# First conv unit reordered, forms loaded in another order, border frames turned in pairs

## Chip, core and metric

The kernel runs on one core of a Trainium2 chip. The core has a matrix engine (TensorE, PE in the profile, with its weight loads as PEld), a vector engine (VectorE, DVE), a scalar engine (ScalarE, ACT), a general engine (GpSimd, POOL) and an engine that mainly issues transfers (SyncE, SP; its transfers show as SPq). Each engine works through its own list of instructions in order and waits on semaphores for the others. Matrix products are gathered in PSUM, everything else lies in SBUF or in the chip's memory (DRAM).

The metric is the device time of one execution in microseconds (us), less is better. Before the change the median of three runs was 2408.08 us (2403.67, 2408.08, 2408.69).

## What is computed

One step of a streaming encoder layer on 576 frames: 512 of a new stream ("prompt") and 64 of a running one ("sample"), width 2048. Cut to what matters here:

```python
hn = rmsnorm(x, g_norm1)
q, k, v, gb, gc, hc = split(hn @ w_in)          # 3 x 1024 for attention, 3 x 1024 for the conv
o_attn = stick_breaking attention of q, k, v (8 heads x 128, with cached keys and values)
u = gc * hc
conv = conv_w[0]*u[t-2] + conv_w[1]*u[t-1] + conv_w[2]*u[t]   # causal, 3 taps, with carried state
o_conv = gb * conv
mix = concat(rmsnorm(o_attn, g_attn_out), rmsnorm(o_conv, g_conv_out))
x = x + mix @ w_out
h2 = rmsnorm(x, g_norm2)
y = x + (silu(h2 @ w_gate) * (h2 @ w_up)) @ w_down            # w_gate, w_up: 2048 x 5632
```

All values are float32, and the outputs are y for both streams, the new keys and values, and the conv states.

## The kernel before

**Splits and units.** A float32 product is made of three matmuls. Each operand is split into a high half (ACT casts it to the type fp32r that PE multiplies) and a low half (DVE subtracts the high half): `split`, L222 to L224. PE then multiplies high by high, low by high and high by low. The 576 frames lie as two halves of 288 columns. From the third conv group on, large projections are done in "units": a 2 x 2 scheme in the manner of Strassen and Winograd, in which weight blocks a11, a12 (first half of the columns of a unit) and a21, a22 (second half) take part in seven products in place of eight. A product `(n, p)` of unit n is 24 matmuls (8 blocks of depth by 3) of 128x128 by 128x288. Its weight operand is a block or a sum of blocks:

- product 1: a11, product 2: a12, product 4: a22
- product 6: s1 - a11 with s1 = a21 + a22, product 5: s1, product 7: a21 - a11
- product 3: a12 less what product 6 used

The frames' operands are sums of the frames' blocks ("forms") made ahead of time. Products 1, 6, 5 and 3 add up in the same PSUM bank psy (`st["y"]`); between them ACT copies the partial sum out (`kept`, L1016: p1 after product 1, u2 after product 6, the copy named acc after product 5). Product 2 gathers in bank z0 (psx), products 7 and 4 in psw. `done` (L1031, L1033) evicts a result on DVE: it adds the kept part and scales by the row scale R1.

**Stages.** Heads (projection and attention), two conv groups in the standard way, then the conv units with number 0 to NCU - 1 = 8 (kinds u, u, b in turn: h, c and gate columns), then eight "output" units from NCU on, which multiply the attention half of the mix by w_out, then the conv half by w_out (`out_proj`), then units of w_gate and w_up, then units of w_down.

**The loop around the change** is over `corder`, the list of products of the conv and output units. In each turn `conv_run` issues product number k, and then `conv_prepare` makes the weight operand of number k + 4: sums on DVE (L975, L976, L977, L979), the high half on ACT, the low half on DVE. For unit 0 the list begins (0,1), (0,2), (1,1), (1,2), (0,6), (0,7), (0,5), (0,3), (0,4), and then (1,6), (1,7), (1,5). Products 1 and 2 of unit 0 are prepared in the group before, and those of unit 1 ahead of the loop. Weights come through three places of 1 MB; when the last sum of a block has been made (after the preparation of product 3 or 4), its place is given free and the next block is called into it (`call_columns`, L943, loads at L956 and L963). In unit 0, the preparation of product 6 makes all three sums at once, s1 into a spare block `cx`.

The order of ACT's and DVE's instructions is normally set by the planner of the tile framework from costs that it estimates; within a `manual_schedule` region an engine takes them in the order of the program's text. `start_mode` is such a region for ACT and DVE. It is opened ahead of the loop and closed after (1,2). `turn_mode` is another one, for SP, from (NCU - 1, 1) on.

**Forms of the output units.** In unit NCU - 1, after its products 6, 7 and 4, pairs of forms of the attention half are loaded (`load_forms`, L1072): forms 1 and 2, then 6 and 7, then 5 and 3, and form 4 last. Between these, in the preparation of (NCU - 1, 3), the place of that unit's first block is given free, and a block of w_out is called into it (L956).

**Stores of y.** In the last stage `take_blocks(d)` gives every down unit d its four blocks of sums, one for each column block c and half of the frames i. When a block is complete, `store_y` turns it: three PE transposes, two of 128 frames and one of the 32 frames left over (the border), a copy on ACT back over the block, a copy of the border into a small tile `obs` (L1688), then the stores. With 32 blocks that makes 32 turns of a border of 32 frames. Each half has its own.

The functions that the change touches:

Of the kernel before, what the change touches and what calls it, by code (L numbers as in the profile page):

```python
# [10 lines left out]
F32 = mybir.dt.float32  # L11
# [83 lines left out]
def tile_hybrid_stream_step(  # L95
# [872 lines left out]
    def conv_prepare(n, p_):  # L968
        st, tt, m = cst.setdefault(n, {"left": 7}), nc.vector.tensor_tensor, NP if n < NCU else NH // 2
        if p_ == 1:  # L970
            _, st["a11"], st["a12"] = cregion[n, 0]
        if p_ == 6:
            _, st["a21"], st["a22"] = cregion[n, 1]
            s1 = st["s1"] = bt["s1"][:, :m]
            tt(out=s1, in0=st["a21"], in1=st["a22"], op=ALU.add)  # L975
            tt(out=st["a21"], in0=st["a21"], in1=st["a11"], op=ALU.subtract)  # L976
            tt(out=st["a11"], in0=s1, in1=st["a11"], op=ALU.subtract)  # L977
        if p_ == 3:
            tt(out=st["a12"], in0=st["a12"], in1=st["a11"], op=ALU.subtract)  # L979
        src = st[{1: "a11", 2: "a12", 3: "a12", 4: "a22", 5: "s1", 6: "a11", 7: "a21"}[p_]]  # L980
# [9 lines left out]
    ft = {}  # L990

    def conv_frames(n, p_, j):
# [611 lines left out]
    acc = {}  # L1604
    down = {}

    def take_blocks(d):

        if d in (0, 1, 3):
            spare_block({0: "z", 1: "t", 3: "ax"}[d])  # L1610
        if d in (0, 3):
            four = [down["z"][:, q, :] for q in (range(4) if d == 0 else range(4, 6))]
            if d:
                four += [down["ax"][:, q, :] for q in range(2)]
        elif d < 3:
            t = down["t"] if d == 1 else ypool.tile([P, 4, HALF], F32, tag=f"y{NP - 1}", name=f"acc{d}")
            four = [t[:, q, :] for q in range(4)]
        elif d < 6:
            four = [pool.tile([P, HALF], F32, tag=tag, name=f"acc{d}", bufs=2)
                    for pool, tag in (((tmp, "y"), (tmp, "r")) if d == 4 else ((tmp, "sq"), (h2pool, "hx")))  # L1620
                    for _ in range(2)]
        else:
            pool, tag = (tmp, "hl") if d == 6 else (rpool, "R")
            two = [pool.tile([P, 2, HALF], F32, tag=tag, name=f"acc{d}", bufs=2) for _ in range(2)]
            four = [t[:, q, :] for t in two for q in range(2)]
        for q, ap in enumerate(four):
            acc[d, q // 2, q % 2] = ap

# [33 lines left out]
    def store_y(n, c, i):  # L1662
# [13 lines left out]
        quick = n == NU - 1  # L1676

        def work():
            yield 4 if quick else 9
            po = misc("pot")[:, : 3 * P]  # L1680
            for q in range(3):
                w = min(P, HALF - q * P)
                nc.tensor.transpose(po[:w, q * P : (q + 1) * P], src[:, q * P : q * P + w], ident)
            yield 0 if quick else 3
            ob = src[:, : 2 * P].rearrange("p (i c) -> p i c", c=P)
            nc.scalar.copy(out=ob, in_=po[:, : 2 * P].rearrange("p (i c) -> p i c", c=P))
            obs = down["pool"].tile([r, P], F32, tag="obs", name="obs", bufs=4)
            nc.scalar.copy(out=obs, in_=po[:r, 2 * P :])  # L1688
            yield 0 if quick else 4
            if i == 0:  # L1690
                nc.sync.dma_start(out=yp[: 2 * P, cs].rearrange("(i p) c -> p i c", p=P), in_=ob)
            else:
                put(f0, ob[:, 0, :])
                put(f0 + P, ob[:, 1, :])
            put(f0 + 2 * P, obs, nc.scalar if quick else nc.sync)

# [79 lines left out]
```

## Time and profile before

| | before |
|---|---|
| median of three runs | 2408.08 us |
| profiled execution, its own time | 2407.74 us |
| span, from its first to its last instruction | 2406.0 us |
| granted TensorE clock, mean | 0.997 |
| PE busy | 2373.6 us (99%) |
| DVE busy | 1898.7 us (79%) |
| ACT busy | 1168.1 us (49%) |
| POOL busy | 279.1 us (12%) |

How to read the lines that follow. A row of the timeline gives the start in us from the span's start, the duration (of the whole run of instructions when they are several), the engine, the line of the kernel, the operation, out<-in by the program's tile names, the shape and the count. In brackets stands how long the engine had been idle, and what released it. A row of the waits gives the engine and line, what it waited for, and the total, number of times and longest, in us. A row of the stretches gives a stretch's length, then each engine's busy time and count, then the granted clock as a share of full speed, the share of the DMA engines that were busy, and GB/s. whl is a pair of high and low halves, raw_a and raw_c are weight blocks, part is a kept partial sum, cv an evicted result.

### The profile page before, as it was taken

How to read it: one execution, taken by the hardware profiler on the slowest of the kernel's cores; microseconds unless marked ns; L12 is line 12 of the kernel's file. 1: busy time of each engine (PE TensorE's matmuls, PEld its weight loads, DVE VectorE, ACT ScalarE, POOL GpSimd, SP SyncE). 2: the span in 40 equal slices, each digit the busy share in tenths (PEclk: the TensorE clock that was granted, in tenths of full speed). 3: DMA queues.
4: the chain of work that ended last, by engine and by line, in shares of the span. 5: the costliest groups of instructions: out<-in, count | busy, mean ns of one | idle time of the engine just before them, and what ended most of it. 6: DMA issues, size and time to landing. Idle time of an engine off the chain costs nothing.

```text
span 2406.0 us, 44164 instructions
## 1 busy us (share of the span) xinstructions
PE 2373.6 (99%) x17825; PEld 2360.9 (98%) x17825; DVE 1898.7 (79%) x2854; ACT 1168.1 (49%) x2099; POOL 279.1 (12%) x384
## 2 busy tenths in 40 slices
PE   8999999989999999999999999999999999999999
PEld 8999999989999999999999999999999999999998
DVE  7767676678887768888888888888888777887875
ACT  6656565444444545444444444444444444444454
POOL 1111111231111120000000000000000001431211
PEclk9999999999999999999999999999999999999999
DMA  7354433584268733444444434534444945885642
GB/s 255 116 153 138 136 118 95 180 285 123 88 206 221 212 120 112 138 145 150 137 133 150 152 117 155 160 113 156 150 129 141 337 137 189 231 233 196 203 128 80
DMA packets 503956, 386.04 MB, mean 160 GB/s; under 512 B 11726, under 2 KB 492872, under 8 KB 503752
## 3 DMA queue, kind: packets, MB, share of 16 engines
q1 hardware_dynamic: 494408, 366.68, 47.8%
q0 software_dynamic: 8624, 16.22, 3.3%
q8 instruction: 139, 2.28, 0.4%
q14 instruction: 65, 0.53, 0.1%
q10 hardware_dynamic: 720, 0.33, 0.0%
HBM read 296.47 MB, written 86.72 MB: 159 GB/s over the span
## 4 chain that ended last, share of the span: by engine, by line
PE 88%; DVE 5%; DMA 3%; ACT 2%; issue 1%; SPq 1%; POOL 0%; ACTq 0%; POOLq 0%; DVEq 0%
PE psy L1526 33%; PE psw L1526 16%; PE pj L214 10%; PE psx L1526 8%; PE psy L1007 6%; PE pjo L214 4%; PE psw L1007 3%; PE pw L1369 2%; PE psx L1007 2%; DMA o_ob<-xt_dram 1%; DVE whl L224 1%; DMA forms<-form_dram 1%; DVE wlo L177 1%; PE z L685 0%; PE po L752 0%
## 5 line engine op out<-in xcount | busy, mean ns | idle before, releaser
L224 DVE TENSOR_TENSOR whl<-raw_a,whl 128x1024 fp32r<-128x1024 f32 (+4 forms) x372 | 391.0, 1051 | 76.4 <-ACT whl L223 74.9
L1526 PE MATMUL psy<-t,whl 128*128 128x288 f32 x2916 | 436.7, 295 | 0.0
L1526 PE MATMUL psy<-h_s,whl 128*128 128x288 f32 x2724 | 410.8, 295 | 1.7 <-ACT part L1536 1.7
L223 ACT CAST whl<-raw_a 128x1024 fp32r<-128x1024 f32 (+4 forms) x372 | 327.0, 881 | 163.9 <-issue 36.6
L1526 PEld LDWEIGHTS psy<-t,whl 128*128 128x128 f32 x2916 | 403.0, 188 | 0.2
L214 PE MATMUL pj<-x,whi 128*128 128x288 f32 x1856 | 398.4, 300 | 0.3 <-DVE x L357 0.3
L1526 PEld LDWEIGHTS psy<-h_s,whl 128*128 128x128 f32 x2724 | 377.4, 188 | 2.2 <-ACT part L1536 2.2
L1526 PE MATMUL psw<-t,whl 128*128 128x288 f32 x2592 | 376.9, 295 | 0.0
L1526 PEld LDWEIGHTS psw<-t,whl 128*128 128x128 f32 x2592 | 353.7, 188 | 0.2
L214 PEld LDWEIGHTS pj<-x,whi 128*128 128x128 f32 x1856 | 307.4, 189 | 1.0 <-DVE x L357 0.6
L214 PE MATMUL pj<-x,wlo 128*128 128x288 f32 x928 | 274.9, 296 | 0.1
L224 DVE TENSOR_TENSOR whl<-raw_b,whl 128x1024 fp32r<-128x1024 f32 (+5 forms) x186 | 194.0, 1043 | 70.1 <-ACT whl L223 69.1
L223 ACT CAST whl<-raw_b 128x1024 fp32r<-128x1024 f32 (+5 forms) x186 | 161.0, 868 | 161.8 <-issue 69.4
L1536 ACT COPY part<-psy 128x288 f32<-128x288 f32 x237 | 94.4, 398 | 267.5 <-PE psy L1526 266.4
L214 PEld LDWEIGHTS pj<-x,wlo 128*128 128x128 f32 x928 | 175.5, 189 | 0.7 <-DVE wlo L424 0.3
L1526 PE MATMUL psx<-h_s,whl 128*128 128x288 f32 x1122 | 164.6, 294 | 0.8 <-DVE gs L1349 0.8
L1526 PEld LDWEIGHTS psx<-h_s,whl 128*128 128x128 f32 x1122 | 154.0, 188 | 1.0 <-ACT form L223 1.0
L223 ACT CAST whl<-s 128x1024 fp32r<-128x1024 f32 (+5 forms) x79 | 70.1, 888 | 100.0 <-PE psw L1526 98.5
L1289 POOL DMA_DIRECT2D hid_dram<-form x3 | 2.2, 748 | 977.9 <-DVE form L224 976.0
L177 DVE TENSOR_TENSOR wlo<-raw_a,whi 128x1024 fp32r<-128x1024 f32 (+1 forms) x80 | 97.0, 1226 | 8.9 <-ACT whi L176 7.8
L214 PE MATMUL pjo<-mixc,whi 128*128 128x288 f32 x512 | 101.7, 294 | 0.0
L176 ACT CAST whi<-raw_a 128x1024 fp32r<-128x1024 f32 (+1 forms) x85 | 85.7, 1024 | 19.4 <-PE pjo L214 9.0
(449 smaller groups left out, 3959.5 us busy)
## 6 DMA issues: line engine op xcount, KB each, us to landing
hid_dram<-form SPq DMA_DIRECT2D x147, 288.0 KB, 2.4
raw_a<-in_w_in_dram SPq DMA_DIRECT2D x41, 1024.0 KB, 5.6
raw_a<-in_w_gate_dram SPq DMA_DIRECT2D x23, 1024.0 KB, 5.8
raw_a<-in_w_up_dram SPq DMA_DIRECT2D x23, 1024.0 KB, 5.4
raw_b<-in_w_gate_dram SPq DMA_DIRECT2D x21, 1024.0 KB, 6.6
raw_b<-in_w_up_dram SPq DMA_DIRECT2D x21, 1024.0 KB, 7.8
h_s<-hid_dram SPq DMA_DIRECT2D x10, 2016.0 KB, 9.7
raw_a<-in_w_out_dram SPq DMA_DIRECT2D x16, 1024.0 KB, 5.7
```

Of the source, the lines that this page charges most:

```text
L176: nc.scalar.copy(out=hi[:, a:b], in_=raw[:, a:b])
L177: lo_eng.tensor_tensor(out=lo[:, a:b], in0=raw[:, a:b], in1=hi[:, a:b].bitcast(F32), op=ALU.subtract)
L214: mm(ps, w_[:, k, csl], x_, start=(k == 0 and n == 0), stop=(k == nk - 1 and n == 2))
L223: nc.scalar.copy(out=hi, in_=src)
L224: (lo_eng or nc.vector).tensor_tensor(out=lo, in0=src, in1=hi.bitcast(F32), op=ALU.subtract)
L1007: mm(ps, whl[:, w_, j, :], x_, start=(start and j == 0 and q == 0), stop=(j == m - 1 and q == 2), skip_group_check=True)
L1289: q.dma_start(out=hid_dram[fp][2 * n - 2 : 2 * n].rearrange("f p t -> p f t"), in_=t.bitcast(F32))
L1369: mm(pss[j, i], w_[:, k, j * P : (j + 1) * P], x_, start=(kk == 0 and k == 0 and n == 0), stop=(kk == 1 and k == 7 and n == 2))
L1526: mm(ps, whl[:, w_, j, :], x_, start=(start and j == 0 and q == 0), stop=(j == len(xs_) - 1 and q == 2), skip_group_check=True)
L1536: nc.scalar.copy(out=t, in_=st["y"])
```

## The change

It has three parts.

1. *Unit 0.* Product (0,7) comes ahead of (0,6) in `corder`. Only (1,1) is prepared ahead of the loop; after product number 1 come the preparations of (1,2) and (0,7), after number 2 that of (0,6), after number 3 those of (0,5) and (0,3), and from then on one each turn as before. Since `conv_run` of (0,2) now stands ahead of these, the eviction of (0,2) stands ahead of the sums in DVE's order. The sums are made otherwise: for (0,7) a21 becomes a21 - a11 in two half blocks, with the cast and low half in two half blocks as well; (0,6) uses s2 = (a21 - a11) + a22, in `cx`; (0,5) uses s1 = s2 + a11, in a11's place. `start_mode` is now closed after (0,5).
2. *Forms.* Forms 1, 2, then 6, 7 are loaded first, then the block of w_out (its place is held back in `held` and called at (NCU - 1, 7)), then form 4 there, and forms 5 and 3 last, after product 4.
3. *Border frames.* `take_blocks` notes in `both[d, c]` the tile that has the two halves of a block behind each other. For these, the half that is complete first leaves its border alone, and the other turns both borders (64 frames) in one transpose, one copy and one store by `put`. In the first half of such a block the 256 frames turned are 0 to 255, in the second half frames 32 to 287 of that half, so that the two borders lie next to each other. Units d = 4 and 5 have their halves in separate tiles and go on as before.

The instruction lists that result, in the neighbourhood of part 1. ACT: high half (1,1), the activations of the conv group's last step (mx, sqm), copy p1 of (0,1), high half (1,2), two half casts of (0,7), copy p1 of (1,1), high halves of (0,6), (0,5), (0,3), (0,4), copy u2 of (0,6), high halves of (1,7), (1,6), copy acc of (0,5), high half of (1,5). DVE: low half (1,1), mx of the conv group, eviction of (0,2), low half (1,2), the two half differences, the two half low halves of (0,7), s2, low half (0,6), eviction of (1,2), s1, low half (0,5), the difference for (0,3), low halves (0,3), (0,4), then unit 1's sums and low halves, and the eviction of (1,1) of unit 0. In part 2, four of ACT's casts of w_out's blocks for unit NCU + 1 stand behind ACT's sums of squares and the copy of the conv state, where they stood ahead of them before. In part 3, twelve of the 32 border transposes, border copies and border stores go (SP has 12 instructions fewer).

```diff
@@ conv_prepare
-        if p_ == 6:
+        if p_ == 7 and n == 0:
+
+            _, st["a21"], st["a22"] = cregion[n, 1]
+            cturn[0] += 1
+            whl = wpool.tile([P, 2, NP, P], F32R, tag=("whi", "wlo")[cturn[0] % 2], name="whl")
+            a21, ks_ = st["a21"], (slice(0, 4), slice(4, 8))
+            for q in ks_:
+                tt(out=a21[:, q], in0=a21[:, q], in1=st["a11"][:, q], op=ALU.subtract)
+                nc.scalar.copy(out=whl[:, 0, q], in_=a21[:, q])
+            for q in ks_:
+                tt(out=whl[:, 1, q], in0=a21[:, q], in1=whl[:, 0, q].bitcast(F32), op=ALU.subtract)
+            coper[n, p_] = whl
+            return
+        if p_ == 6 and n == 0:
+
+            s2 = st["s2"] = bt["s1"]
+            tt(out=s2, in0=st["a21"], in1=st["a22"], op=ALU.add)
+        elif p_ == 6:
...
+        if p_ == 5 and n == 0:
+            st["s1"] = st["a11"]
+            tt(out=st["s1"], in0=st["s2"], in1=st["a11"], op=ALU.add)
+            st["a11"] = st["s2"]
...
-            if n < NCU or (n, 4 - p_) not in cregion:
+            if (n, p_) == (NCU - 1, 3):
+                held.append(q)
+            elif n < NCU or (n, 4 - p_) not in cregion:
                 call_columns([q])
@@ the loop
-    corder = [(0, 1), (0, 2), (1, 1), (1, 2), (0, 6), (0, 7), (0, 5), (0, 3), (0, 4), (1, 6), (1, 7), (1, 5)]
+    corder = [(0, 1), (0, 2), (1, 1), (1, 2), (0, 7), (0, 6), (0, 5), (0, 3), (0, 4), (1, 6), (1, 7), (1, 5)]
...
-    for p_ in (1, 2):
-        conv_prepare(1, p_)
+    conv_prepare(1, 1)
...
-        if (n, p_) == (1, 2):
+        if (n, p_) == (0, 5):
             start_mode.close()
-        if k_ + 4 < len(corder):
-            conv_prepare(*corder[k_ + 4])
+
+        for q in ((), (3, 4), (5,), (6, 7))[k_] if k_ < 4 else range(k_ + 4, min(k_ + 5, len(corder))):
+            conv_prepare(*corder[q])
...
-            if p_ == 4:
+            if p_ == 7:
+                call_columns(held)
                 load_forms(apool.tile([P, NH // 2, 2, HALF], F32R, tag="oa", name="forms0"), 0, 4)
@@ store_y
+        lone = (d, c) not in both
+        k0 = 0 if lone or i == 0 else r
+        rest = None
+        if lone:
+            rest = src[:, 2 * P :], f0 + 2 * P
+        elif (d, c) in one:
+            rest = both[d, c].rearrange("p i t -> p (i t)")[:, 2 * P : 2 * P + 2 * r], 2 * P
+        one[d, c] = i
...
-            for q in range(3):
-                w = min(P, HALF - q * P)
-                nc.tensor.transpose(po[:w, q * P : (q + 1) * P], src[:, q * P : q * P + w], ident)
+            for q in range(2):
+                nc.tensor.transpose(po[:, q * P : (q + 1) * P], src[:, k0 + q * P : k0 + (q + 1) * P], ident)
+            if rest:
+                nr = rest[0].shape[1]
+                nc.tensor.transpose(po[:nr, 2 * P :], rest[0], ident)
...
-            put(f0 + 2 * P, obs, nc.scalar if quick else nc.sync)
+            if rest:
+                put(rest[1], obs[:nr], nc.scalar if quick else nc.sync)
```

More of the change, by code (lines that the diff above doesn't have):

```diff
@@ L1604, in tile_hybrid_stream_step @@
     acc = {}
+    both, one = {}, {}
     down = {}
@@ L1611, in take_blocks @@
         if d in (0, 3):
-            four = [down["z"][:, q, :] for q in (range(4) if d == 0 else range(4, 6))]
-            if d:
-                four += [down["ax"][:, q, :] for q in range(2)]
+            z = down["z"]
+            two = [z[:, 0:2, :], z[:, 2:4, :]] if d == 0 else [z[:, 4:6, :], down["ax"]]
         elif d < 3:
             t = down["t"] if d == 1 else ypool.tile([P, 4, HALF], F32, tag=f"y{NP - 1}", name=f"acc{d}")
-            four = [t[:, q, :] for q in range(4)]
+            two = [t[:, 0:2, :], t[:, 2:4, :]]
         elif d < 6:
@@ L1621, in take_blocks @@
                     for _ in range(2)]
+            for q, ap in enumerate(four):
+                acc[d, q // 2, q % 2] = ap
+            return
         else:
@@ L1624, in take_blocks @@
             two = [pool.tile([P, 2, HALF], F32, tag=tag, name=f"acc{d}", bufs=2) for _ in range(2)]
-            four = [t[:, q, :] for t in two for q in range(2)]
-        for q, ap in enumerate(four):
-            acc[d, q // 2, q % 2] = ap
+        for c, t in enumerate(two):
+            both[d, c] = t
+            for i in range(2):
+                acc[d, c, i] = t[:, i, :]
     def spare_block(name):
@@ L1692, in work @@
             else:
-                put(f0, ob[:, 0, :])
-                put(f0 + P, ob[:, 1, :])
-            put(f0 + 2 * P, obs, nc.scalar if quick else nc.sync)
+                put(f0 + k0, ob[:, 0, :])
+                put(f0 + k0 + P, ob[:, 1, :])
+            if rest:
+                put(rest[1], obs[:nr], nc.scalar if quick else nc.sync)
         pipe.spawn(work())
```

9 lines of the change are left out of this document (5 added, 4 removed).

## Prediction

> **What bounds the kernel now.** First the busy shares on the page, then who TensorE waited for.
>
> ```profile
> span 2406.0 us, 44164 instructions
> ...
> PE 2373.6 (99%) x17825; PEld 2360.9 (98%) x17825; DVE 1898.7 (79%) x2854; ACT 1168.1 (49%) x2099; POOL 279.1 (12%) x384
> ```
>
> TensorE (PE) is busy in 2373.6 of 2406.0 us, so a change can give only what it takes out of PE's own work or of the 32 us in which PE stands. Next, PE's longest waits around the first conv unit (500 to 620 us) and around the change from conv to output units (700 to 760 us).
>
> ```profile
> PE psx L1007 <- DVE cv L1031: 5.3, 1, 5.3
> ...
> PE psw L1007 <- DMA forms<-form_dram: 1.1, 1, 1.1
> PE psy L1007 <- ACT whl L223: 1.0, 1, 1.0
> ```
>
> The long one is the wait of product (1,2) for the eviction of (0,2), for both use PSUM bank z0. The timeline shows why it came late and what followed:
>
> ```profile
> 511.30 2.95 DVE L224 TENSOR_TENSOR whl<-raw_c,whl 128x1024 fp32r<-128x1024 f32 x2
> 511.37 0.29 PE L1007 MATMUL psy<-x,whl 128*128 128x288 f32 x1
> ...
> 512.35 0.81 POOL L511 TENSOR_TENSOR acc_c<-acc_c,sqm 128x288 f32<-128x288 f32 x1 [1.38 <-ACT sqm L510]
> ...
> 512.56 3.34 PE L1007 MATMUL psy<-x,whl 128*128 128x288 f32 x23 [0.90 <-DVE whl L224]
> 514.17 0.51 DVE L524 SCALAR_TENSOR_TENSOR mx<-gbr,vec,mx 128x288 fp32r<-128x288 f32 x1
> 514.60 1.21 DVE L975 TENSOR_TENSOR cx<-raw_a 128x1024 f32<-128x1024 f32 x1
> ...
> 518.42 1.99 ACT L223 CAST whl<-raw_a 128x1024 fp32r<-128x1024 f32 x2 [5.86 <-DVE raw_a L977]
> ...
> 520.64 0.45 DVE L1031 TENSOR_TENSOR cv<-psx,part 128x288 f32<-128x288 f32 x1
> 521.13 0.46 DVE L1033 TENSOR_TENSOR cv<-cv,R 128x288 f32<-128x288 f32 x1
> ...
> 521.24 5.56 PE L1007 MATMUL psx<-x,whl 128*128 128x288 f32 x24 [5.34 <-DVE cv L1031]
> ...
> 526.64 3.33 PE L1007 MATMUL psy<-xs_t,whl 128*128 128x288 f32 x24
> ...
> 527.92 1.22 DVE L224 TENSOR_TENSOR whl<-raw_a,whl 128x1024 fp32r<-128x1024 f32 x1
> 529.17 3.84 SPq L963 DMA_DIRECT2D raw_a<-in_w_in_dram  x2
> ...
> 534.84 1.23 DVE L975 TENSOR_TENSOR cx<-raw_a 128x1024 f32<-128x1024 f32 x1 [2.22 <-DMA raw_a<-in_w_in_dram]
> ...
> 536.35 0.40 ACT L1016 COPY part<-psy 128x288 f32<-128x288 f32 x1 [5.00 <-PE psy L1007]
> ...
> 536.80 3.43 PE L1007 MATMUL psy<-x,whl 128*128 128x288 f32 x24 [0.49 <-ACT part L1016]
> ...
> 538.86 1.05 ACT L223 CAST whl<-raw_c 128x1024 fp32r<-128x1024 f32 x1 [0.41 <-DVE raw_c L977]
> ...
> 540.08 3.33 PE L1007 MATMUL psw<-xs_t,whl 128*128 128x288 f32 x24
> 540.24 1.22 DVE L224 TENSOR_TENSOR whl<-raw_c,whl 128x1024 fp32r<-128x1024 f32 x1
> ...
> 543.25 3.33 PE L1007 MATMUL psy<-xs_t,whl 128*128 128x288 f32 x24
> ```
>
> (0,2) was done when (1,1) began (511.37), but VectorE (DVE) made four sums and a low half (514.60 to 520.64) before it read the bank. PE stood from 515.90 to 521.24, and the next 24 matmuls took 5.56 us where 24 take 3.33. The stretches of the trace say what the extra 2.2 us are; the columns are the stretch, its length, busy time and count for PE, weight load, DVE, ACT and POOL, then the granted clock:
>
> ```profile
> 512.00:516.00 4.00, 3.34 (x23) 3.10 (x23) 3.96 (x5) 0.56 (x2) 1.55 (x2) 1.00 0.94 293
> ...
> 518.00:521.00 3.00, 0.00 (x0) 0.00 (x0) 2.96 (x4) 1.99 (x2) 0.00 (x0) 0.69 1.05 386
> 521.00:526.00 5.00, 4.76 (x20) 4.79 (x21) 2.82 (x4) 1.34 (x2) 0.00 (x0) 0.50 1.09 390
> 526.00:528.00 2.00, 2.00 (x17) 2.00 (x17) 0.99 (x3) 1.05 (x1) 0.00 (x0) 1.00 1.09 389
> ```
>
> The granted clock fell to a half during the wait and stayed there to 526. So the region lost 0.9 + 5.3 + 2.2 + 0.5, about 9 us. A second thing is to be seen: unit 1's second weight block is loaded into the place that the low half of (0,3) frees (527.92 + 1.22 = 529.14; load issued 529.17), and DVE's first sum on it starts 5.67 us later, at 534.84. The sums give (1,6) its operand (high half 538.86, low half 540.24 to 541.46), and PE needs it at 543.25. The slack of unit 1 against that load is thus 1.8 us, whatever happens to the stall before it.
>
> **First unit, step by step.** DVE's and ScalarE's (ACT's) order in the changed program is fixed by hand up to the end of (0,5). Durations: a sum or low half of 1024 columns 1.22 us, a high half 1.05, an eviction with its scaling 0.9 (520.64 to 521.50), copy of a partial sum 0.40 with PE going on 0.45 after its start (536.35 to 536.80). Half blocks:
>
> ```profile
> 698.01 0.68 DVE L976 TENSOR_TENSOR raw_a<-raw_a 128x512 f32<-128x512 f32 x1
> ...
> 705.58 0.62 ACT L223 CAST whl<-raw_a 128x512 fp32r<-128x512 f32 x1
> ```
>
> The low half of (1,1) still starts at 511.30 and PE at 512.56, so the wait of 0.9 stays. DVE then does the last step of the conv group (mx, 0.51 alone; beside a POOL add I take 0.9) to 513.3, and evicts (0,2) to 514.2. The bank is free before 515.90: the wait of 5.3 us and its slow matmuls go. Low half of (1,2) to 515.4; (1,2) runs from 515.90, (0,7) from 519.1. The two half differences, ACT's two half casts and the two half low halves follow one another to 518.0; PE needs them at 519.1. s2 to 519.2, high half of (0,6) to 520.3, low half to 521.6, needed at 522.3. PE ends (0,6) at 525.4, without a stall. So far 7.5 us are won.
>
> What is late next: (0,5) adds into the same psy bank as (0,6), whose copy u2 must come first. Before, (0,7) lay between them. In the changed order ACT reaches u2 behind the high halves of (0,5), (0,3) and (0,4). DVE: eviction of (1,2) to 522.4, s1 523.6, [ACT high half 524.7], low half (0,5) 526.0, difference for (0,3) 527.2, [ACT 528.2], low half (0,3) 529.6. ACT casts (0,4) to 529.2 and copies u2; PE starts (0,5) at 529.6. It has stood 4.2 us.
>
> Then (0,3) needs the copy of (0,5)'s sum, and in ACT's order that copy stands behind the high halves of (1,7) and (1,6), so behind the load of unit 1. Its place is freed at 529.6, 0.4 later than before, so the load does not come earlier. First sum at 529.6 + 5.67 = 535.3; the second load is now issued about 1.2 us behind the first where it was over 3 behind (DVE's next low half frees it), for which I add 0.3 (bounds 0, if loads are served in order, and 1.5, if two of 1 MB share the engines). Three sums at 1.25 to 539.3, high half of (1,6) to 540.4, copy, and PE starts (0,3) at 540.8, where it was 536.80: +4.0 us. PE has stood since about 533.
>
> That wait is longer than the one that halved the clock, so (0,3) should run slowly as (1,2) did: 5.56 instead of 3.43, +2.1. (0,4) starts 6.1 us later than the 540.08 of before, and behind it the view of the waits up to 620 has nothing that could take this back. Bounds: below, +4.0 alone if the clock holds; above, +4.0 + 1.2 + 3.4.
>
> By the Trainium skill (TensorE: Matmul & The Clock Gate, "What's actually happening") the clock goes to a half after one idle window of about 3.4 us that runs freely, and back after one busy window. By that rule a wait of over 6.8 us always holds a whole idle window, and the loss after it is half of 3.4 to 6.8 us, an estimate of 1.7 to 3.4 where the row has 2.1; the sum would be 2412.6 to 2414.3. The trace agrees as far as it goes (0.50 from about 519.1, full again at 526).
>
> **Forms in another order.** The chain and the timeline at the change to the output units:
>
> ```profile
> 698.93 0.99 SPq L1072 DMA_DIRECT2D forms<-form_dram  x2
> ...
> 705.58 0.37 SPq L956 DMA_DIRECT2D raw_a<-in_w_out_dram  x1
> ...
> 706.00 13.39 SPq L1072 DMA_DIRECT2D forms<-form_dram  x5
> ...
> 717.90 1.78 PE L1007 MATMUL psy<-forms,whl 128*128 128x288 f32 x12
> ...
> 718.91 0.43 ACT L223 CAST sqg<-acc_c 128x288 fp32r<-128x288 f32 x1
> ...
> 730.30 1.83 PE L1007 MATMUL psw<-forms,whl 128*128 128x288 f32 x12 [1.14 <-DMA forms<-form_dram]
> ```
>
> Forms 6 and 7 waited on SP behind a weight load that was issued at 705.58; now they go ahead of it, and form 4 ahead of forms 5 and 3. The same bytes pass, and the loads end about 1 us earlier at most, so form 3, now last, lands near 729. The planner answered by putting the four casts from the first in its path, unit NCU+1 product 1, behind ACT's sums of squares and state copy: cast about 718.6, low half 719.9, so that product starts at 720.0 instead of 717.90 (+2.1). Later waits (1.0 at 727.3 and 1.1 at 730.3) shrink in turn: (0.5 of the copy stays) product 3 ends the later of both, near 730.7, and product 4 starts there instead of 730.30: +0.4. Bounds -1.1 (the form's wait goes, nothing new) and +2.1 (nothing is given back).
>
> **Border frames.** Twelve of 32 turns of border frames go (24 blocks pair up, 8 stay alone), with twelve ACT copies and twelve stores. PE pays for the turns:
>
> ```profile
> 2377.87 0.33 PE pot L1683 x3
> ...
> L1688 ACT COPY obs<-pot x32: 247/250/253, 2289.8 to 2401.9; 32x128 f32<-32x128 f32 x32
> ```
>
> 0.33 for three is 0.11 each, 12 x 0.11 = 1.3 us, on PE's path, since PE is full there. The copies (12 x 0.25 us of ACT) and the stores on SP lie beside PE and I cost them at nothing; the last block (unit 4) stays alone, so the tail after the last matmul is the same. Bounds -1.3 and -1.9 (two waits of PE on these copies and evictions, 0.3 each, may go too).
>
> **Sum.** The profiled execution's own time is 2407.74 us, 0.3 below the median of 2408.08. 2407.74 + 6.1 + 0.4 - 1.3 = 2412.9; rounded up for small handovers that I left out, 2413.0 us, 0.2% above the median: the forecast lies on the line between no change and slower (0.2%, 4.8 us, is about what a measurement can tell here, for the three runs of before span 5 us).
>
> **Rivals.** (A) Not slower: the clock does not fall, or rises at once, in the wait before (0,3). Place: that wait; it decides when PE's rest is too short for the fall, between the 0.90 us before 512.56 that left the clock at 1.00 and the 5.3 us that halved it. The sum is then 2413.0 - 2.1 = 2410.9. Against it: the rest is near 7.7 us. (B) Faster: ACT's copies do not hold PE, if the hardware's order leaves them earlier than I read. Then (0,5) to (0,4) run from 526 to 536, but (1,6) still waits for the load: low half at 541.6 instead of PE's 543.25, so at most 1.65 us are won, and with the borders and forms 2407.74 - 1.65 + 0.4 - 1.3 = 2405.2, still inside 0.2%. Even the stall's full removal can't bring the gain one expects from 9 us. (C) Clearly slower: both loads of weights share the engines (+1.2) and the output units do not give back their 2.1 us (+1.7): 2415.9. For it: ACT's new order there puts every later cast behind PE's own progress. Against: product 4 had a wait on a form to absorb it.
>
> **Chances.** My forecast 0.50, with its own range 2411.5 to 2414.5, half on each side of the line; A 0.18; B 0.06; C 0.22; something unseen that helps 0.04. That makes slower 0.25 + 0.22 and a little of A's upper end, 0.49; within 0.2% 0.46; faster 0.05. The range 2408 to 2418 takes A and C with half the spread of the runs of before on the outside (2410.9 - 2.5 = 2408.4 and 2415.9 + 2.5 = 2418.4) and leaves out B.
>
> **What would show it.** In the changed kernel's trace: no wait of psx at (1,2), and full clock through 525; PE idle from about 525.4 to 529.6, then again from 533 to 540.8, both put down to ACT's copy; the granted clock at 0.50 after the second; the load of unit 1 issued near 529.6. In the output units a wait of about 2 us before product 1 of the second unit, and less before product 4. Twelve turns fewer under pot. The prediction is wrong if (0,3) starts before 539, which would mean that the copy does not stand behind the load, or if the loads of unit 1 are issued well before 529.

## The result, and the profile after

The changed kernel takes 2412.68 us (median of ten runs, 2410.23 to 2416.09), the kernel before 2406.85 us (ten runs, 2403.67 to 2408.69): a ratio of 1.0027, 95% interval 1.0017 to 1.0036. It is slower by about 6 us. The profiled execution took 2411.92 us, its span is 2410.2.

On the page of the changed kernel PE is as busy as before, and its busy time hardly moved (2374.3 against 2373.6 us):

```profile
span 2410.2 us, 44104 instructions
...
PE 2374.3 (99%) x17813; PEld 2362.0 (98%) x17813; DVE 1897.7 (79%) x2856; ACT 1166.1 (48%) x2088; POOL 281.8 (12%) x384
```

Most of the loss is in rests of PE and in matmuls that run slowly behind them; a smaller part comes in the later conv units, of which more below. The first row is PE's waits of the changed kernel from 500 to 620 us, where before had 5.3 for DVE's eviction; the second is the longest of those from 700 to 760 us, where before had 1.1 for a form and 1.0 for ACT's cast (the columns are the total, the number of times and the longest):

```profile
PE psy L1032 <- ACT part L1041: 10.0, 2, 5.9
...
PE psy L1032 <- ACT whl L223: 1.3, 1, 1.3
```

The timeline of the changed kernel around the first unit (line numbers move with each kernel's edits; here L1007 is L1032):

```profile
503.34 3.33 PE L1032 MATMUL psy<-x,whl 128*128 128x288 f32 x24
...
513.22 3.33 PE L1032 MATMUL psx<-x,whl 128*128 128x288 f32 x24
516.39 3.33 PE L1032 MATMUL psw<-xs_t,whl 128*128 128x288 f32 x24
519.56 3.33 PE L1032 MATMUL psy<-xs_t,whl 128*128 128x288 f32 x24
...
524.66 1.99 ACT L223 CAST whl<-raw_a 128x1024 fp32r<-128x1024 f32 x2 [2.50 <-DVE raw_a L1000]
...
526.55 0.39 ACT L1041 COPY part<-psy 128x288 f32<-128x288 f32 x1
526.99 2.23 SPq L963 DMA_DIRECT2D raw_a<-in_w_in_dram  x2
...
527.00 4.98 PE L1032 MATMUL psy<-x,whl 128*128 128x288 f32 x24 [4.11 <-ACT part L1041]
532.66 1.22 DVE L992 TENSOR_TENSOR cx<-raw_a 128x1024 f32<-128x1024 f32 x1 [4.57 <-DMA raw_a<-in_w_in_dram]
...
535.31 1.04 ACT L223 CAST whl<-raw_a 128x1024 fp32r<-128x1024 f32 x1 [8.37 <-DVE raw_a L993]
...
536.44 1.04 ACT L223 CAST whl<-raw_c 128x1024 fp32r<-128x1024 f32 x1
537.39 0.39 ACT L1041 COPY part<-psy 128x288 f32<-128x288 f32 x1
...
537.84 5.11 PE L1032 MATMUL psy<-x,whl 128*128 128x288 f32 x24 [5.86 <-ACT part L1041]
542.78 3.34 PE L1032 MATMUL psw<-xs_t,whl 128*128 128x288 f32 x24
```

(1,2), (0,7) and (0,6) now follow one another without a stall (513.22, 516.39, 519.56). Then the copy u2 comes only at 526.55, behind two casts that take 1.99 us together and that waited for DVE, and PE rests 4.1 us. The copy of (0,5)'s sum comes at 537.39, behind the casts at 535.31 and 536.44, which wait for DVE's sums on a block that was called at 526.99; PE rests 5.9 us. The stretches of the changed kernel give the clock (the third number from the right):

```profile
529.00:532.00 3.00, 2.98 (x15) 2.75 (x13) 0.00 (x0) 0.00 (x0) 0.00 (x0) 0.62 1.08 320
...
537.80:541.00 3.20, 3.16 (x13) 3.17 (x14) 2.91 (x4) 0.00 (x0) 0.00 (x0) 0.50 0.00 0
...
725.00:727.20 2.20, 2.17 (x12) 2.18 (x13) 1.77 (x3) 0.75 (x2) 0.00 (x0) 0.69 1.07 402
727.20:729.70 2.50, 2.50 (x13) 2.50 (x13) 0.69 (x1) 0.92 (x2) 0.00 (x0) 0.59 1.05 381
```

It is at half behind both rests, and again at 725 to 729 us, at the change to the output units. The values 0.62, 0.69 and 0.59 are means of stretches in which the clock changes between 0.50 and 1.00; from 537.8 to 541.0 it is 0.50 throughout.

The start of the conv units differs by up to 4.7 us from one profiled execution to another (from 501.2 to 506.0 us over all kernels), through the stages ahead of it, which none of these edits touches. So stages are compared by distances. For before, the rows are these, in the same order as the columns of the table: the first matmul of (0,1), of (1,5), of (NCU,1), of the first 36 in the output units, and of the first turn of y.

```profile
505.02 3.33 PE L1007 MATMUL psy<-x,whl 128*128 128x288 f32 x24
...
549.60 9.68 PE L1007 MATMUL psy<-x,whl 128*128 128x288 f32 x72
...
714.61 1.75 PE L1007 MATMUL psy<-forms,whl 128*128 128x288 f32 x12
...
735.14 4.92 PE L1007 MATMUL psy<-forms,whl 128*128 128x288 f32 x36
...
2288.73 0.49 PE L1683 MATMUL pot<-ident,acc_z 128*128 128x128 f32 x3
```

| us, profiled execution | (0,1) to (1,5) | to (NCU,1) | to the 36 | to the first turn | to the end |
|---|---|---|---|---|---|
| before | 44.58 | 165.01 | 20.53 | 1553.59 | 117.27 |
| changed | 48.97 | 167.22 | 22.07 | 1552.68 | 115.92 |
| difference | +4.39 | +2.21 | +1.54 | -0.91 | -1.35 |

With the start of (0,1) 1.68 us earlier in this execution, the differences add up to the 4.2 us by which the spans differ. How far a stage moves without an edit in it is seen over all thirteen profiles: the way from the 36 to the first turn took 1551.5 to 1554.0 us, so the -0.91 can't be told from that spread; in the kernels with the first unit as before, the first column was 44.2 to 44.6 where the eviction had not been moved, and the second 165.0 to 165.9; with the forms as before, the third was 20.3 to 20.9.

### The profile page after: what moved, and what is told of

Read it like the earlier page. It is cut to its first block, busy times and chain, and to the rows that moved or that the text cites. A ratio compares the mean times of both kernels' runs of the same rounds, so it can differ in the third digit from the quotient of the medians.

```text
span 2410.2 us, 44104 instructions
## 1 busy us (share of the span) xinstructions
PE 2374.3 (99%) x17813; PEld 2362.0 (98%) x17813; DVE 1897.7 (79%) x2856; ACT 1166.1 (48%) x2088; POOL 281.8 (12%) x384
## 4 chain that ended last, share of the span: by engine, by line
PE 83%; DVE 8%; DMA 4%; ACT 3%; issue 2%; POOL 1%; SPq 0%; ACTq 0%; DVEq 0%; POOLq 0%
PE psy L1552 33%; PE psw L1552 16%; PE pj L214 11%; PE psx L1552 8%; PE pjo L214 4%; PE psy L1032 3%; DVE whl L224 2%; PE pw L1395 2%; PE psw L1032 2%; DMA raw_a<-in_w_in_dram 1%; DMA o_ob<-xt_dram 1%; DMA raw_c<-in_w_in_dram 1%; PE psx L1032 1%; ACT whl L223 1%; PE po L752 0%
## 5 line engine op out<-in xcount | busy, mean ns | idle before, releaser
L1552 PE MATMUL psx<-h_s,whl 128*128 128x288 f32 x1122 | 165.0, 295 | 0.0
L1032 PE MATMUL psy<-x,whl 128*128 128x288 f32 x648 | 91.6, 302 | 10.0 <-ACT part L1041 10.0
```

The lines of the kernel that those rows point to most:

```text
L1032: mm(ps, whl[:, w_, j, :], x_, start=(start and j == 0 and q == 0), stop=(j == m - 1 and q == 2), skip_group_check=True)
L1552: mm(ps, whl[:, w_, j, :], x_, start=(start and j == 0 and q == 0), stop=(j == len(xs_) - 1 and q == 2), skip_group_check=True)
```

## The experiments

Times are medians, each with a ratio to the kernel before from the same chip and, in parentheses, the 95% interval of that ratio. The median of the kernel before was 2404.8 to 2405.6 us beside these runs, and 2406.85 beside the changed kernel, so the ratios compare better than the times. "Distance" is that of the first column of the table.

**The three parts alone.** The first unit's part:

```diff
-        if p_ == 6:
+        if p_ == 7 and n == 0:
...
-        if (n, p_) == (1, 2):
+        if (n, p_) == (0, 5):
             start_mode.close()
...
+        for q in ((), (3, 4), (5,), (6, 7))[k_] if k_ < 4 else range(k_ + 4, min(k_ + 5, len(corder))):
```

> The first unit's part alone (with its order of products, sums and preparations), the forms and borders as before. My theory: it carries nearly all of the loss. In the changed kernel (1,6) starts 4.4 us later, counted from the start of (0,2), than before, so 2406.85 + 4.4 = 2411.3, or up to 2413 if the later wait of 1.1 us on a low half in a following unit belongs to it too; PE waits of about 4 us before (0,5) and 6 us before (0,3), both for ACT's copy. Rival: the unit's part is even or a gain (at most 2407), and the loss comes from the new place of the forms and of the w_out block; then no such waits matter for the end.

2412.06 us, ratio 1.0028 (1.0018 to 1.0039). The distance is 49.00 (44.58 before), and the way on to (NCU,1) 167.29 (165.01): the unit's part by itself is as slow as the whole change.

The forms' part:

```diff
+            if (n, p_) == (NCU - 1, 3):
+                held.append(q)
...
-            if p_ == 4:
+            if p_ == 7:
+                call_columns(held)
                 load_forms(apool.tile([P, NH // 2, 2, HALF], F32R, tag="oa", name="forms0"), 0, 4)
```

> The order of the forms and the held block of w_out alone. In the changed kernel the output units cost 1.5 us more than before (from the first product of the first output unit to the fourth unit's), with ACT's four casts behind the sums of squares, so I expect 2406.85 + 1.5 = 2408.4 with a wait of over 1 us of psy for ACT's cast and no wait for a form. My prediction had +0.4 here, with bounds -1.1 and +2.1. Rival: the forms are a gain of about 1 us (2405.8), and the cost of that stage in the changed kernel came with the delay of the first unit.

2407.04 us, ratio 1.0004 (0.9995 to 1.0013). In time alone that is no measurable change, but the stage of the output units took 22.26 us against 20.53, with waits at the same place as in the changed kernel:

```profile
718.55 0.40 PE L1011 MATMUL psy<-forms,whl 128*128 128x288 f32 x1 [1.47 <-ACT whl L223]
719.34 2.64 PE L1011 MATMUL psy<-forms,whl 128*128 128x288 f32 x11 [0.39 <-DVE whl L224]
721.78 2.40 PE L1011 MATMUL psx<-forms,whl 128*128 128x288 f32 x12
724.01 1.75 PE L1011 MATMUL psy<-forms,whl 128*128 128x288 f32 x12
```

From 719.34 to 724.01 there are 23 matmuls in 4.67 us, where 23 at full speed take 3.0 (24 follow one another in 3.17, from 513.22 to 516.39 above). That is 1.6 us of the stage's 1.7: the waits themselves are paid back by waits that are gone further on (for ACT's cast and for a form), the slow clock behind them is not.

The borders' part:

```diff
+        lone = (d, c) not in both
+        k0 = 0 if lone or i == 0 else r
...
-            for q in range(3):
+            for q in range(2):
...
+            if rest:
+                put(rest[1], obs[:nr], nc.scalar if quick else nc.sync)
```

> The paired border frames alone. Twelve turns of 0.11 us fewer on PE: 2406.85 - 1.3 = 2405.5, at most -1.9. Rival: nothing (2406.8), if PE's turns stood where PE waited anyway, or a loss, if a store now comes later than the last one did.

2402.15 us, ratio 0.9987 (0.9978 to 0.9996). The way from the first turn of y to the end is 115.87 us against 117.27: -1.4, as forecast. It was 115.87 to 115.99 in all eight kernels with paired borders and 117.27 to 117.48 in the five others, so this term is known to 0.2 us, while the median of the whole carries the other stages' variation with it.

**The copies ahead of the casts.**

```diff
-        for q in ((), (3, 4), (5,), (6, 7))[k_] if k_ < 4 else range(k_ + 4, min(k_ + 5, len(corder))):
+        for q in ((), (3, 4), (5,), (6,), (), (7, 8), (9, 10))[k_] if k_ < 7 else range(k_ + 4, min(k_ + 5, len(corder))):
```

> The changed kernel with the preparations of (0,3) and (0,4) moved behind the copy u2 of (0,6), and those of unit 1's products 6 and 7 behind the copy of (0,5); all else as changed. My theory (ACT's order holds PE twice): the wait of 4.1 us before (0,5) and that of 5.9 us before (0,3) shrink to 0.5 each, (0,4) runs about 9 us earlier, and what is late next is unit 1's load, which is issued no earlier (about 14 us after (1,2) starts): (1,6) then waits about 5 us for its low half and runs slowly behind it, so 7.0 - 1.7 = 5.3 us are won of the 10: 2412.7 - 5.3 = 2407.4. Rival 1 (the copies are not what holds PE): no change, 2412.7. Rival 2 (the load has slack): all 10 us come back, 2402.7 or less.

2405.74 us, ratio 1.0001 (0.9992 to 1.0010). The distance fell from 48.97 to 44.99 with this one line:

```profile
505.96 3.33 PE L1032 MATMUL psy<-x,whl 128*128 128x288 f32 x24
...
526.17 4.25 PE L1032 MATMUL psy<-x,whl 128*128 128x288 f32 x24 [0.49 <-ACT part L1041]
530.90 3.47 PE L1032 MATMUL psy<-x,whl 128*128 128x288 f32 x24 [0.49 <-ACT part L1041]
534.21 3.33 PE L1032 MATMUL psw<-xs_t,whl 128*128 128x288 f32 x24
541.30 0.61 PE L1032 MATMUL psy<-xs_t,whl 128*128 128x288 f32 x1 [3.75 <-ACT whl L223]
543.15 4.79 PE L1032 MATMUL psy<-xs_t,whl 128*128 128x288 f32 x23 [1.24 <-DVE whl L224]
```

Both long waits for the copy are down to 0.49, and the rest of PE has moved to (1,6), which waits 3.75 us for its high half and 1.24 for its low half, behind the load, and then runs at half clock. (0,4) came 11 us earlier than in the changed kernel, counted from (0,1), and 4.0 of them reached (1,5), where I had 5.3. The first rival falls, the second too.

**The eviction alone moved, in the kernel before.**

```diff
-        if k_ + 4 < len(corder):
-            conv_prepare(*corder[k_ + 4])
+        for q in ((), (4, 5))[k_] if k_ < 2 else range(k_ + 4, min(k_ + 5, len(corder))):
+            conv_prepare(*corder[q])
```

> The kernel before with one edit: the preparations of (0,6) and (0,7) come after product (0,2) and its eviction, not before; order of products, sums, forms and borders as before. My theory: the wait of 5.3 us at (1,2) and its slow matmuls go; two shorter waits come before (0,6) (about 0.8 for its high half, 1.3 for its low half); the low half of (0,3) ends about 3.8 us earlier, so unit 1's load is issued that much earlier, and (1,6) starts at PE's own pace, 5.5 us earlier than before; 3.8 if the two short waits halve the clock for a while. So 2405.6 - 3.8 to - 5.5 = 2400.1 to 2401.8. Rival (case B of the prediction: unit 1 waits for its load whatever the stall does): at most 1.7 us, 2403.9.

2401.91 us, ratio 0.9988 (0.9979 to 0.9997); distance 40.68, 3.9 less than before. The rests are now short, and the clock falls all the same:

```profile
518.44 0.40 PE L1007 MATMUL psy<-xs_t,whl 128*128 128x288 f32 x1 [1.34 <-ACT whl L223]
519.70 4.84 PE L1007 MATMUL psy<-xs_t,whl 128*128 128x288 f32 x23 [0.87 <-DVE whl L224]
```

Rests of 1.34 and 0.87 us, and 23 matmuls take 4.84 us, where 23 took 3.34 before (at 512.56). The load of unit 1 was issued at 523.45, 19.8 us behind (0,1) (24.2 before), and (1,6) did not wait. So the stall's removal was worth more here than the 1.65 us that case B of the prediction allowed, since the load moves with it when the preparations follow earlier.

**The load earlier.** In the changed kernel, with copies ahead of casts:

```diff
             tt(out=s2, in0=st["a21"], in1=st["a22"], op=ALU.add)
+            st["s1"] = st["a21"]
+            tt(out=st["s1"], in0=s2, in1=st["a11"], op=ALU.add)
+            st["a11"] = s2
...
         if p_ == 5 and n == 0:
-            st["s1"] = st["a11"]
-            tt(out=st["s1"], in0=st["s2"], in1=st["a11"], op=ALU.add)
-            st["a11"] = st["s2"]
-        if p_ == 3:
+            tt(out=st["a12"], in0=st["a12"], in1=st["a11"], op=ALU.subtract)
+        if p_ == 3 and n:
...
+        for q in ((), (3, 4), (5, 6), (7,), (), (8,), (9, 10))[k_] if k_ < 7 else range(k_ + 4, min(k_ + 5, len(corder))):
```

> The changed kernel, with s1 made right after s2 (in a21's place), the difference for (0,3) made ahead of (0,5)'s low half, and the copies u2 and acc ahead of the casts that follow them, so that the place for unit 1's second block comes free about 10.5 us after (1,2) starts (13.8 in the changed kernel). My theory (after the copies, the load is what is late): first sum on the block 5.7 us after the issue, (1,6) starts 31 us after (0,1) began, with a wait of under 1 us, where it was 38.2 before and 42.6 in the changed kernel. With the forms' +1.4 and the borders' -2 to -3.4 that is 2405.6 - 7.1 + 1.4 - 2.5 = 2397.4. Rival (another thing holds unit 1, such as DVE's queue): (1,6) no earlier than in the run with the copies moved (about 36 us behind (0,1)), 2405.

2399.05 us, ratio 0.9976 (0.9968 to 0.9985). The load was issued 10.2 us after (1,2) began, as expected, but (1,6) started 32.5 us behind (0,1), not 31, waited 0.33 and 1.16, and ran at half clock (23 matmuls in 4.84 us); the distance is 41.94, and the time 1.7 us above my figure. One thing in this run was not looked for. In the output units PE rested 1.26 and 0.39 us as in the changed kernel, and the matmuls behind ran at full speed:

```profile
713.16 0.40 PE L1033 MATMUL psy<-forms,whl 128*128 128x288 f32 x1 [1.26 <-ACT whl L223]
713.95 1.74 PE L1033 MATMUL psy<-forms,whl 128*128 128x288 f32 x11 [0.39 <-DVE whl L224]
715.53 1.75 PE L1033 MATMUL psx<-forms,whl 128*128 128x288 f32 x12
```

The same place in the changed kernel:

```profile
724.24 0.40 PE L1032 MATMUL psy<-forms,whl 128*128 128x288 f32 x1 [1.26 <-ACT whl L223]
725.02 2.37 PE L1032 MATMUL psy<-forms,whl 128*128 128x288 f32 x11 [0.39 <-DVE whl L224]
727.19 2.68 PE L1032 MATMUL psx<-forms,whl 128*128 128x288 f32 x12
```

The same rests cost 1.3 us more in one of the two (22.07 against 20.81 for the stage). So rests of this length do not always halve the clock.

**Form 4 ahead, the block of w_out in its old place.**

```diff
-            if p_ == 4:
+            if p_ == 7:
                 load_forms(apool.tile([P, NH // 2, 2, HALF], F32R, tag="oa", name="forms0"), 0, 4)
```

> The kernel before, with only form 4 loaded ahead of forms 5 and 3; the block of w_out stays where it was, ahead of forms 6 and 7. My theory: what moved ACT's four casts behind the sums of squares is the held block of w_out, since the planner takes its load to be later. Here they stay in place: no wait of 1.3 to 1.5 us for them, and the wait of 1.1 us for form 4 goes, but one for form 3 may take its place: 2405.6 - 0 to - 1.1 = 2404.5 to 2405.6. Rival (the order of forms 4, 5, 3 is what costs): as the forms alone, 2407.0 with the wait for ACT's cast.

2406.73 us, ratio 1.0012 (1.0003 to 1.0020). No wait for the casts: it is the held block that puts them behind the sums of squares, as expected. The time came out on the rival's side, through another wait, since form 5 is used first and now lands last but one:

```profile
727.67 2.95 PE L1007 MATMUL psy<-forms,whl 128*128 128x288 f32 x12 [2.16 <-DMA forms<-form_dram]
```

12 matmuls in 2.95 us for 1.75: again a rest (2.16 us) and the half clock behind it.

**PE kept busy in the waits.** The changed kernel, with 16 and 26 spare matmuls:

```diff
+    def fill(n):
+        x = conv_frames(0, 3, 0)[0]
+        ps = misc("fill")[:, :HALF]
+        for q in range(n):
+            mm(ps, x[:, :P], x, start=(q == 0), stop=(q == n - 1), skip_group_check=True)
+
     def conv_run(n, p_):
+        if (n, p_) in ((0, 5), (0, 3)):
+            fill(16 if p_ == 5 else 26)
```

> The changed kernel with spare matmuls on PE in the two waits: 16 before (0,5) and 26 before (0,3), on frames that lie ready, into a bank that nobody reads; nothing waits for them. My theory: the resting of PE is what halves the granted clock, so with PE kept busy (0,5) and (0,3) take near 3.3 us in place of 4.98 and 5.11. (0,5)'s gain goes into the wait before (0,3), whose end is set by the load; (0,3)'s is won: 2412.7 - 1.7 = 2411.0. Rival (the clock falls for another reason, such as DVE's or the transfers' load): both stay near 5, and the time stays at 2412.7 or rises by what the spare matmuls run over the wait.

2409.96 us, ratio 1.0022 (1.0013 to 1.0031), with rests of 2.01 and 2.33 us left, and both products still at 4.98 us: this run could not tell the theories apart. So the next has 30 and 43 (the edit is against the run with 16 and 26):

```diff
-            fill(16 if p_ == 5 else 26)
+            fill(30 if p_ == 5 else 43)
```

> The changed kernel with more spare matmuls on PE: 30 before (0,5) and 43 before (0,3), so that they last about as long as the two waits (4.1 and 5.9 us). In the run with 16 and 26, rests of 2.0 and 2.3 us were left, and the clock still halved behind each. My theory (resting of about 2 us is enough to halve the clock): with under 0.5 us of rest left, (0,5) and (0,3) run at full clock, 3.4 us in place of 4.98; (0,3)'s gain is kept, 2412.7 - 1.7 = 2411.0. Rival (the matmuls behind a wait are slow for another reason than PE's rest): both stay at 4.98 at a granted clock of 0.50.

2408.32 us, ratio 1.0015 (1.0006 to 1.0024). Its timeline:

```profile
527.83 3.44 PE L1032 MATMUL psy<-x,whl 128*128 128x288 f32 x24 [0.18 <-ACT part L1049]
531.10 5.83 PE L1040 MATMUL fill<-x 128*128 128x288 f32 x43
538.63 3.48 PE L1032 MATMUL psy<-x,whl 128*128 128x288 f32 x24 [1.70 <-ACT part L1049]
```

Its stretches, of which the second is the rest left before (0,3):

```profile
527.80:531.10 3.30, 3.27 (x24) 3.27 (x25) 1.13 (x1) 0.00 (x0) 0.00 (x0) 1.00 0.60 177
...
537.00:538.60 1.60, 0.00 (x0) 0.00 (x0) 1.60 (x3) 1.50 (x3) 0.00 (x0) 1.00 0.00 0
538.60:541.90 3.30, 3.27 (x24) 3.27 (x25) 2.91 (x4) 0.00 (x0) 0.00 (x0) 1.00 0.02 5
```

(0,5) takes 3.44 and (0,3) 3.48 us at a clock of 1.00, beside the same copies and the same loads, with 0.18 and 1.70 us of rest left (I had meant under 0.5). So it is PE's rest that halves the clock, and not DVE's or the transfers' work. The distance is 47.83 against 48.97, although the load was issued 0.5 us later behind (0,1) than in the changed kernel (24.2 against 23.7), which makes 1.7 us for (0,3)'s clock; (0,5)'s went into the wait behind it. The ratio's interval is too wide to price this in the whole time.

**Two versions meant to beat both.** The early version's sums for units 0 and 1, (1,7) ahead of (1,6), paired borders, forms as before:

```diff
-    corder = [(0, 1), (0, 2), (1, 1), (1, 2), (0, 7), (0, 6), (0, 5), (0, 3), (0, 4), (1, 6), (1, 7), (1, 5)]
+    corder = [(0, 1), (0, 2), (1, 1), (1, 2), (0, 7), (0, 6), (0, 5), (0, 3), (0, 4), (1, 7), (1, 6), (1, 5)]
...
-        if p_ == 7 and n == 0:
+        if p_ == 7 and n < 2:
```

> The early version of the first unit (s1 right after s2, copies ahead of casts), the same order and sums for unit 1 as well, with (1,7) in half blocks ahead of (1,6), the paired borders, and the forms as in the kernel before. My theory: what held unit 1 in the early version was the three sums and two casts between the load and (1,6)'s low half; with (1,7) first, one half sum and one half cast stand there, and neither (1,7) nor (1,6) waits. (1,5) then starts 38.4 us behind (0,1), where it is 44.6 before, 49.0 in the changed kernel and 41.9 in the early version. With the borders' -1.4: 2404.8 - 6.2 - 1.4 = 2397.2. Rival (the load itself lands too late, or the clock falls at another place): 41 us or more, 2399.5 or above.

2398.74 us, ratio 0.9976 (0.9966 to 0.9986). The distance is 37.57, better than expected, with no wait above 0.5 us up to there; but the way on to (NCU,1) took 167.46 us against 165.01, so a third of the gain (2.5 of 7.0 us) was given back. The second version is the eviction's edit with the paired borders, in the kernel before:

```diff
+        for q in ((), (4, 5))[k_] if k_ < 2 else range(k_ + 4, min(k_ + 5, len(corder))):
+            conv_prepare(*corder[q])
...
+        lone = (d, c) not in both
```

> The kernel before with the eviction of (0,2) ahead of the sums (as in the run with that edit alone) and the paired borders; forms and order of products as before. Terms add up: 2404.8 - 3.6 - 1.4 = 2399.8. Rival (the gains share a wait, so that they don't add): no better than the eviction alone, 2401.9.

2399.14 us, ratio 0.9974 (0.9963 to 0.9985): the two gains add. The plain one is as fast as the one with all the sums rearranged.

**Where 2 us are lost in the later units.** In the changed kernel nearly all of the 2.2 us lie at two products. Up to (6,6), the first that is late, both kernels take 104.72 us from (1,5). There PE waits for the low half of the weights, and again, for 0.20 us, at (8,6), both by the timeline:

```profile
649.27 1.23 DVE L992 TENSOR_TENSOR cx<-raw_a 128x1024 f32<-128x1024 f32 x1 [3.35 <-DMA raw_a<-in_w_in_dram]
...
658.43 3.31 PE L1032 MATMUL psy<-xs_t,whl 128*128 128x288 f32 x23 [1.11 <-DVE whl L224]
```

DVE's first sum on unit 6's second block comes 7.8 us ahead of the start of (6,6), at 657.03, after a wait of 3.35 us for that block. Before, it came 9.8 us ahead (644.53 against 654.32), after a wait of 1.33, and PE did not wait. The product takes 1.4 us longer in consequence, and (8,6) with the two behind it 0.8.

DVE's waits for blocks of w_in between 546 and 700 us, for before, the changed kernel and the version with two units:

```profile
DVE cx L975 <- DMA raw_a<-in_w_in_dram: 4.4, 3, 2.0
DVE cx L975 <- DMA raw_c<-in_w_in_dram: 1.9, 2, 1.5
```

```profile
DVE cx L992 <- DMA raw_a<-in_w_in_dram: 10.2, 4, 3.4
...
DVE cx L992 <- DMA raw_c<-in_w_in_dram: 5.1, 3, 2.3
```

```profile
DVE cx L995 <- DMA raw_a<-in_w_in_dram: 10.8, 4, 3.0
DVE cx L995 <- DMA raw_c<-in_w_in_dram: 5.6, 3, 2.2
```

6.3, 15.3 and 16.4 us. With one profile of each kernel, there are two groups: with 6.3 to 8.3 us of such waits (before, the forms, form 4 alone, the borders, the eviction alone and with borders, the early version) this stage takes 165.0 to 165.9 us, with 12.0 to 16.4 (the others of which the first unit was changed) 166.1 to 167.5. Within a profile such as the changed kernel's the waits come in every unit. The groups lie close (165.9 and 166.1 us). What decides into which group a kernel falls stays open: PE's earlier or later arrival alone does not, since both the changed kernel and the version with two units are in the second group. No run held DVE's order in the later units fixed.

## Why the prediction was right

The forecast was 2413.0 us and the result is 2412.68; the range (2408 to 2418) and the direction hold, and the two rests of PE came where they were forecast. That the figure came out within 0.3 us was luck: the terms were off by up to 2.2 us either way and cancel.

- *The stall goes.* Right: no wait at (1,2), clock 1.00, (0,7) and (0,6) without a rest.
- *u2 behind three casts, a rest of 4.2 us.* Right: 4.11. That this rest alone halves the clock was not forecast: (0,5) took 4.98 us. It cost nothing there, because the wait behind it ends with the load.
- *The copy of (0,5)'s sum behind unit 1's load.* Right, and shown by the copies' run. I had set 539 as the time before which (0,3)'s start would speak against it; it started at 537.84, but (0,1) began 1.68 us earlier than in before's profile, and on before's scale that is 539.5. The load, forecast near 529.6, was called at 526.99, on that scale 528.7. The term was +4.0 and measured +2.7 (537.84 - 503.34 against 536.80 - 505.02). What was missing: the wait of 0.9 at (1,1) that I had kept was not there in this execution, and the sums followed at 532.66, 533.92 and 535.18 with no wait for the second load (the 0.3 I had added). The first sum came 5.67 us after the issue, the very figure of before.
- *The slow product.* +2.1 forecast, +1.7 measured (5.11 against 3.43). The clock's fall is due to PE's rest, as the run with 30 and 43 spare matmuls showed; rival A falls. So at (0,4) the sum was +6.1 and came to +4.4.
- *"behind it the view of the waits up to 620 has nothing that could take this back."* This is the step that did not hold. Nothing took the loss back, but the sum had no term for new waits behind 620 us, and 2.2 us were lost between (1,5) and (NCU,1), at (6,6) and around (8,6). The two errors cancel: 4.4 + 2.2 = 6.6 against 6.1.
- *Forms.* +0.4 forecast, +1.5 measured, within the bounds (-1.1, +2.1). The mechanism was read rightly: the casts behind the sums of squares delay the first product of unit NCU + 1 (by 1.4, forecast 2.1), and the later waits for a cast and for a form (0.97 and 1.14) become one of 0.49 in return. What was missing is the clock: rests of 1.26 and 0.39 us halved it in this execution, and 1.47 and 0.39 in that of the forms alone. Where it did not fall (the copies, the early version, both runs with spare matmuls) the stage took 20.8 to 21.1 us, 0.2 to 0.5 over before. That agrees with my figure, but kernels with the forms as before reach 20.9 as well. Rival C's first half (a dearer second load) was not seen; its second half, +2.1 in place of +0.4, is nearer in size than my figure, but by another cause: the waits were given back, the slow clock was not.
- *Borders.* -1.3 forecast, -1.4 measured.
- *Case B.* For the changed order it was priced rightly: with the copies out of the way (1,6) waited for the load, and the distance was 44.99, no gain on 44.58. But "even the stall's full removal can't bring the gain one expects from 9 us" took the load's place as given: with the eviction first and the sums as before, the load moves forward too, and 3.9 us are won in the distance; the version with two units won 7.0.

The rule that I set beside the row (the Trainium skill, TensorE: Matmul & The Clock Gate, "What's actually happening") would have the clock fall after a window of about 3.4 us without work. Its length fits: the half clock lasted about 3.4 us in the run with 16 and 26 spare matmuls (from 528.1 to 531.5), and twice that at the 5.3 us rest of before (519.1 to 526). But rests of 2.0 to 2.3 us were enough in three places here (both of the run with 16 and 26 spare matmuls, and form 4's), and so were two rests of 1.7 us in sum behind each other in the changed kernel, so a rest need not fill a window.

## What to carry to other kernels

In an order fixed by hand, look on each engine at what the small copy that frees a bank stands behind, not only at the operation that was late before: here one line that put two copies of 0.4 us ahead of four casts was worth 4 us of its stage. Where the stall that goes had covered a load, ask first when the load's place comes free. The smallest edit that removes the wait (the eviction first) won 0.12% by itself, while the larger rearrangement around it lost 0.28%.

## What the runs showed of the hardware that was not expected

The granted clock halved after rests of PE of only about 2 us, and the same pair of rests (1.26 and 0.39 us) did or did not halve it from one kernel to another. Rests that left it at 1.00 were up to 1.70 us long (in the run with 30 and 43 spare matmuls, at 537 us), and a pair of 1.69 and 0.39 us left it there too (in the run with 16 and 26, at the change to the output units). So the length of the rests alone does not decide.

Half-microsecond stretches of the changed kernel put the changes of its clock at 527.9, 531.3, 534.7 and 541.5 us, and again at 725.8 and 729.2. These lie on one raster of 3.41 us (4 steps from 527.9 to 541.5, 58 to 725.8). Where a rest falls against the raster may be the rest of the answer; no run moved a rest against it, so that is not shown.

Where the clock fell ahead of 23 or 24 matmuls, of which 24 take 3.33 us at full clock, they took 4.7 to 6.1 us, a loss of 1.5 to 2.8 us each time. The largest came behind the 5.3 us rest that the kernel before has: 5.56 us in its own profile, 6.1 in those of the forms and of the borders alone.
